# Layer 0 attention: three in five head pairs' probabilities transposed in fp32 on TensorE, stages of the pipeline reordered

## The chip, the cores and the metric

The kernel runs on one core of one Trainium2 chip. The metric is the device time of one execution in microseconds (us). A run's profile adds a trace of one execution: every instruction of TensorE (PE, with its weight loads as PEld), VectorE (DVE), ScalarE (ACT), GpSimd (POOL) and SyncE (SP, which here only issues DMAs), and the DMA packets.

## The reference, cut to what matters

Two layers of a diffusion backbone over 1024 latent tokens and 256 context tokens, width 1024. Layer 0 mixes by windowed attention with a sink (A, 8 heads, 2 key heads) and by 2-D neighbourhood attention (B, 8 heads); layer 1 by two other attentions; each layer ends in a mixture of experts. The change touches only the softmax and the value product of layer 0:

```python
s_ctx = einsum(q, k_c) * scale                      # 256 context keys
s_loc = einsum(q, k_local) * scale (+ bias in B)    # masked local keys
p_ctx, p_loc = joint_softmax([s_ctx, s_loc])        # in A also the sink's score
o = einsum(p_ctx, v_c) + einsum(p_loc, v_local)
```

The result has to be near to fp32, so the kernel keeps a number as two fp16 numbers, a high part and the rest (low part), and makes a product of three matmuls (high by high, high by low, low by high).

## The kernel before, in words

**Items.** `attn_l0` goes through six units: 0 and 1 are A with four heads each, 2 to 5 are B with two heads each. An item is one block of 128 queries of one head; a unit has 10 query blocks, so A has 80 items and B has 80. In A an item has 256, 512 or 640 keys, in B 256, 768 or 896 (256 of them context). Two neighbouring heads of a block are a pair: 80 pairs in all.

**One item's way** (`attn_unit`). `qk` (L679 to L682): scores into a PSUM buffer S of 1024 fp32; there are two (`ps_s`). `soft` (L702 to L730): maximum on DVE, exponentials on ACT into Pt (fp32, SBUF, two buffers), then their fp16 high part into Ps by an ACT copy (L730). `low` (L737): the low part, Pt minus high, into Ps; `low_eng` gives 4 items in 10 to POOL and 6 to DVE. After the second head of a pair, one DMA transposes all of Ps (high and low of both heads) into PT, issued by SP (L739). `pv` (L183 to L185 in `mm3`): three matmuls a key block, PT by values, into O; after a block's last head, DVE multiplies O by the reciprocal sums (L771), and ACT, POOL and a DMA store it.

**Order.** `pipelined` lets an item enter each step: at step i it emits qk of item i, pv of i-5, low of i-2 and soft of i-1. Beside it `interleave` emits the next unit's projection (`proj_unit`: products into ps_proj, its own DMA transposes at L628), the layer's modulation products (`ada`: L314, L317, L331), and B's bias tables (L502); in unit 5 instead of the projection the output mixer (`py`). The Tile framework's scheduler then sets a fixed order on each engine from this and from what depends on what; on the chip every engine goes through its row in that order, and an instruction that waits holds all behind it.

**DMA.** One hardware queue, issued by SP, carries weight loads and all transposes.

Of the kernel before, what the change touches and what calls it, by code (L numbers as in the profile page):

```python
# [12 lines left out]
F32 = mybir.dt.float32  # L13
# [55 lines left out]
def drain(g):  # L69
    for _ in g:  # L70
        pass


def pipelined(items, stages):
    n, depth = len(items), len(stages)
    st = [None] * n
    for i in range(n + depth - 1):
        for s in (0, *range(depth - 1, 0, -1)):
            j = i - s
            if 0 <= j < n:  # L80
                st[j] = stages[s](items[j], st[j])
        yield
# [362 lines left out]
def attn_l0(K, moe):  # L445
    nc, tc = K.nc, K.tc
    with ExitStack() as outer:
# [5 lines left out]
        ps_o = K.pool("l0pso", 2, PSUM, ctx)  # L453
# [55 lines left out]
        with ExitStack() as c0:  # L509
# [11 lines left out]
            for half, groups in ((0, ((8, 2, 1),)), (1, ((8, 2, 1), (0, 4, 0), (4, 4, 0)))):  # L521
                drain(K.ada([(0, half), (0, 2 + half)], wa, ps_p, 8, 3, 2, ps_o))
# [109 lines left out]
        def attn_unit(u):  # L632
# [53 lines left out]
            def soft(it, S):  # L686
# [14 lines left out]
                if isA:  # L701
# [4 lines left out]
                    nc.scalar.activation(Pt[:, :nk], S[:, :nk], AF.Exp, bias=nmh, scale=ESC,  # L706
                                         accum_out=dd[:, 0, h:h + 1])
                else:
# [10 lines left out]
                    nc.vector.tensor_scalar(nmh, mm, -ESC, LNSP, op0=ALU.mult, op1=ALU.add)  # L719
                    nc.scalar.activation(Pt[:, nl:nk], S[:, nl:nk], AF.Exp, bias=nmh, scale=ESC,  # L720
# [4 lines left out]
                if h % 2 == 0:  # L725
                    st_t[t, "Ps"] = pring.tile([P, 4 * 896], F16, name="Ps")
                    st_t[t, h] = tring.tile([P, 28, P], F16, name="PT")
                Ps, PT = st_t[t, "Ps"], st_t[t, h - h % 2]
                a = (h % 2) * 2 * nk
                nc.scalar.activation(Ps[:, a:a + nk], Pt[:, :nk], AF.Copy)  # L730
                return Pt, Ps, PT, a, nk

            def low(it, s):
                Pt, Ps, PT, a, nk = s
                w = 2 * nk
                h = it[1]
                K.low_eng().tensor_sub(Ps[:, a + nk:a + w], Pt[:, :nk], Ps[:, a:a + nk])  # L737
                if h % 2:
                    nc.sync.dma_start_transpose(out=PT[:, :2 * w // P, :], in_=Ps[:, :2 * w])  # L739
                return PT[:, a // P:(a + w) // P]  # L740

            def pv(it, PT):
# [4 lines left out]
                if h == 0:  # L747
                    st_t[t, "O"] = ps_o.tile([P, nh, 64], F32, name="O")
                O = st_t[t, "O"]
# [33 lines left out]
            same = lambda i, s: s  # L783
            yield from pipelined(items, [qk, soft, low, same, same, pv])
# [1270 lines left out]
```

## Time and profile before

| | |
|---|---|
| median of the runs | 3305.45 us |
| fastest run | 3302.15 us |
| profiled execution | 3305.77 us |
| its span in the trace | 3304.0 us (1.8 us lie outside) |
| first scores of layer 0 to last exponentials | about 107 to 788 us, a fifth of the span |
| PE, DVE, ACT, POOL busy over the span | 2616.3, 2599.6, 1976.2, 1000.7 us |

A busy PE is not a PE at its peak: a matmul's row lasts until its result is out, while the next may have begun. "Idle before" is the time that an engine stood still ahead of a group, and the names behind the arrow are what ended it. Lines are those of the kernel before, except in the passages of the order of the changed kernel.

### The profile page before, as it was taken

What the parts mean: (1) busy time and instruction counts of PE and PEld (TensorE: products, weight loads), DVE (VectorE), ACT (ScalarE), POOL (GpSimd) and SP (SyncE); (2) the same over time, 40 slices, a digit from 0 to 9 for tenths busy, and PEclk for the clock granted to TensorE, in tenths of its full rate; (3) what the DMA queues carried; (4) which work ended last, traced back from release to release, by engine and by line L of the source; (5) the groups of instructions that cost most, each with busy time, mean ns of one, the idle gap of its engine ahead of it and who ended that gap; (6) DMA issues with size and microseconds to landing.
All of it is one profiled execution on the core that took longest, in us unless ns stands there. A gap on an engine that the chain in (4) does not pass through costs nothing. (4 is left out here: it accounts for less than half of the span.)

```text
span 3304.0 us, 74455 instructions
## 1 busy us (share of the span) xinstructions
PE 2616.3 (79%) x30127; PEld 1777.7 (54%) x30127; DVE 2599.6 (79%) x4496; ACT 1976.2 (60%) x2949; POOL 1000.7 (30%) x652
## 2 busy tenths in 40 slices
PE   7888889968579989897467777877868579988886
PEld 3545445434267777775245555554534367776662
DVE  6777777778887768887667776778877897889987
ACT  5557777654456656676345655556653565656664
POOL 0123233232342212121432232222221463234443
PEclk8989999979789999999679998999978689999998
DMA  7789898789769889998648999655457589999996
GB/s 238 165 170 190 188 211 186 167 204 221 245 242 336 324 325 367 362 383 328 205 108 148 171 161 183 127 101 101 102 134 201 192 324 343 354 361 379 383 378 255
DMA packets 879159, 790.05 MB, mean 239 GB/s; under 512 B 689397, under 2 KB 719365, under 8 KB 878805
## 3 DMA queue, kind: packets, MB, share of 16 engines
q1 hardware_dynamic: 846981, 714.26, 74.9%
q0 software_dynamic: 26336, 69.85, 6.4%
q8 instruction: 239, 3.92, 0.5%
q10 hardware_dynamic: 5488, 1.09, 0.2%
q14 instruction: 115, 0.94, 0.1%
HBM read 565.85 MB, written 64.55 MB: 191 GB/s over the span
## 5 line engine op out<-in xcount | busy, mean ns | idle before, releaser
L375 DVE SCALAR_TENSOR_TENSOR arena<-arena 128x2048 f16<-128x2048 f32 (+4 forms) x439 | 917.8, 2112 | 175.1 <-ACT arena L374 165.6
L374 ACT ACTIVATE arena<-arena 128x2048 f16<-128x2048 f32 (+4 forms) x439 | 748.7, 1725 | 318.3 <-DMA arena<-in_w_gate_up_dram 195.0
L1364 PE MATMUL pg<-arena 128*128 128x72 f16 (+4 forms) x4736 | 633.3, 210 | 102.8 <-DVE arena L1351 80.4
L1366 PE MATMUL pg<-arena 128*128 128x72 f16 (+4 forms) x4736 | 629.9, 210 | 23.1 <-DVE arena L375 20.3
L1365 PE MATMUL pg<-arena 128*128 128x72 f16 (+4 forms) x4736 | 631.0, 210 | 14.8 <-DVE arena L1351 7.3
L183 PEld LDWEIGHTS <-arena 128*128 128x128 f16 (+1 forms) x3488 | 344.3, 103 | 341.0 <-DMA arena<-arena 128.4
L1365 PEld LDWEIGHTS <-arena 128*128 128x128 f16 x4736 | 473.0, 102 | 69.9 <-issue 66.0
L1366 PEld LDWEIGHTS <-arena 128*128 128x128 f16 x4736 | 472.4, 102 | 52.5 <-DVE arena L375 31.6
L1364 PEld LDWEIGHTS <-arena 128*128 128x128 f16 x4736 | 473.0, 102 | 34.0 <-ACT arena L374 21.4
L184 PEld LDWEIGHTS <-arena 128*128 128x128 f16 (+1 forms) x3488 | 344.3, 103 | 188.0 <-issue 96.2
L1381 POOL DMA_INDIRECT y_d<-arena,rt_sidx x74 | 233.9, 3161 | 615.8 <-ACT arena L1394 310.0
L185 PEld LDWEIGHTS <-arena 128*128 128x128 f16 (+1 forms) x3488 | 344.4, 103 | 129.0 <-issue 22.2
L183 PE MATMUL O<-arena 128*128 128x64 f16 (+1 forms) x1744 | 229.0, 208 | 129.9 <-DMA arena<-arena 98.6
L185 PE MATMUL O<-arena 128*128 128x64 f16 (+1 forms) x1744 | 228.7, 208 | 0.0
L184 PE MATMUL O<-arena 128*128 128x64 f16 (+1 forms) x1744 | 228.4, 208 | 0.0
L1774 POOL TENSOR_TENSOR arena<-arena 128x1280 f16<-128x1280 f32 x57 | 151.6, 2660 | 246.3 <-issue 174.8
L1755 ACT ACTIVATE arena<-S,arena 128x1280 f32<-128x1280 f32 x128 | 169.2, 1322 | 92.8 <-DVE arena L1753 80.6
L1344 POOL DMA_INDIRECT arena<-h_d,rt_gidx x74 | 144.2, 1948 | 233.4 <-PE pt L1350 173.1
L1752 DVE TENSOR_REDUCE arena<-S 128x1 f32<-128x1280 f32 x128 | 189.5, 1482 | 27.4 <-PE S L185 16.6
L195 PE MATMUL py<-arena 128*72 128x512 f16 (+4 forms) x592 | 184.1, 392 | 19.3 <-ACT arena L1376 14.2
L197 PE MATMUL py<-arena 128*72 128x512 f16 (+4 forms) x592 | 182.6, 390 | 0.0
L199 PE MATMUL py<-arena 128*72 128x512 f16 (+4 forms) x592 | 180.6, 386 | 0.0
(390 smaller groups left out, 6262.8 us busy)
## 6 DMA issues: line engine op xcount, KB each, us to landing
arena<-in_w_gate_up_dram SPq DMA_DIRECT2D x256, 1024.0 KB
arena<-in_w_down_dram SPq DMA_DIRECT2D x128, 1024.0 KB
arena<-in_w_ada_dram SPq DMA_DIRECT2D x96, 512.0 KB
arena<-y_d SPq DMA_DIRECT2D x36, 512.0 KB
x_d<-arena POOLq DMA_DIRECT2D x18, 512.0 KB, 3.5
h_d<-arena SPq DMA_DIRECT2D x18, 512.0 KB
arena<-x_d SPq DMA_DIRECT2D x18, 512.0 KB
arena<-in_x_dram SPq DMA_DIRECT2D x16, 512.0 KB
```

The source lines that it names most:

```text
L183: mm(ps, lh, rh, start=first, stop=False)
L184: mm(ps, lh, rl, start=False, stop=False)
L185: mm(ps, ll, rh, start=False, stop=last)
L195: mm(ps[:, o], lh, rh[:, o], start=first, stop=False)
L197: mm(ps[:, o], lh, rl[:, o], start=False, stop=False)
L374: nc.scalar.activation(wh, raw, AF.Copy, scale=scale)
L375: nc.vector.scalar_tensor_tensor(wl, raw, scale, wh, op0=ALU.mult, op1=ALU.subtract)
L1364: mm(pg[:, m, :n], wh, xh, start=k == 0 and m % 4 == 0, stop=False)
L1365: mm(pg[:, m, :n], wh, xl, start=False, stop=False)
L1366: mm(pg[:, m, :n], wl, xh, start=False, stop=k == 7 and m % 4 == 3)
L1381: self.K.nc.gpsimd.indirect_dma_start(out=self.K.y_d[self.l], out_offset=bass.IndirectOffsetOnAxis(ap=sidx, axis=0), in_=y[:n], in_offset= ...
L1752: nc.vector.reduce_max(mx[:, 0:1], S[:, :TOK], axis=AX.X)
```

## The change

Of every five pairs two keep the DMA (`by_dma`), three are transposed by TensorE: `turn` writes the transposes of Pt, in fp32, over the item's own scores in S; `high` copies S to PT as fp16 on ACT; `low` subtracts, on DVE, the high part from S and writes the low part to PT. In the pairs that keep the DMA, low is on POOL always. `soft` is cut in two, `peak` (maximum) and `soft` (exponentials), and the steps are emitted in a new order: at step i transposes of i-1, qk of i, pv of i-4, high of i-1, peak of i, low of i-1, soft of i. O is no longer a ring of two tiles but two halves of one tile (`sums`); the modulation's transposes have a pool of their own (`ps_t`).

```diff
@@ attn_l0
-        ps_o = K.pool("l0pso", 2, PSUM, ctx)
+        ps_t = K.pool("l0pst", 1, PSUM, ctx)
+        sums = K.pool("l0pso", 1, PSUM, ctx).tile([P, 2, 4, 64], F32, name="O")
...
-            def soft(it, S):
+            def peak(it, S):
...
-                    nc.scalar.activation(Pt[:, :nk], S[:, :nk], AF.Exp, bias=nmh, scale=ESC,
-                                         accum_out=dd[:, 0, h:h + 1])
...
+                return S, Pt
+
+            def soft(it, s):
+                S, Pt = s
...
+                if isA:
+                    nc.scalar.activation(Pt[:, :nk], S[:, :nk], AF.Exp, bias=nmh, scale=ESC,
+                                         accum_out=dd[:, 0, h:h + 1])
+                else:
...
                 if h % 2 == 0:
+                    st_t[t, h] = tring.tile([P, 28, P], F16, name="PT")
+                PT, a = st_t[t, h - h % 2], (h % 2) * 2 * nk
+                if not by_dma(it):
+                    return S, Pt, None, PT, a, nk
+                if h % 2 == 0:
                     st_t[t, "Ps"] = pring.tile([P, 4 * 896], F16, name="Ps")
...
+            def by_dma(it):
+                pair = (u * NT * nh + items.index(it)) // 2
+                return pair * 4 % 10 < 4
+
+            def turn(it, s):
+                S, Pt, Ps, PT, a, nk = s
+                if Ps is None:
+                    for j in range(0, nk, P):
+                        nc.tensor.transpose(S[:, j:j + P], Pt[:, j:j + P], K.id32)
+
+            def high(it, s):
+                S, Pt, Ps, PT, a, nk = s
+                if Ps is None:
+                    nc.scalar.activation(PT[:, a // P:(a + nk) // P].rearrange("p a n -> p (a n)"), S[:, :nk], AF.Copy)
 
             def low(it, s):
-                Pt, Ps, PT, a, nk = s
+                S, Pt, Ps, PT, a, nk = s
                 w = 2 * nk
-                h = it[1]
-                K.low_eng().tensor_sub(Ps[:, a + nk:a + w], Pt[:, :nk], Ps[:, a:a + nk])
-                if h % 2:
-                    nc.sync.dma_start_transpose(out=PT[:, :2 * w // P, :], in_=Ps[:, :2 * w])
+                if Ps is None:
+                    h_, l_ = (PT[:, (a + b) // P:(a + b + nk) // P].rearrange("p a n -> p (a n)") for b in (0, nk))
+                    nc.vector.tensor_sub(l_, S[:, :nk], h_)
+                else:
+                    nc.gpsimd.tensor_sub(Ps[:, a + nk:a + w], Pt[:, :nk], Ps[:, a:a + nk])
+                    if it[1] % 2:
+                        nc.sync.dma_start_transpose(out=PT[:, :2 * w // P, :], in_=Ps[:, :2 * w])
...
             def pv(it, PT):
...
-                if h == 0:
-                    st_t[t, "O"] = ps_o.tile([P, nh, 64], F32, name="O")
-                O = st_t[t, "O"]
+                O = sums[:, order.index(t) % 2, :nh]
...
-            same = lambda i, s: s
-            yield from pipelined(items, [qk, soft, low, same, same, pv])
+            n, st = len(items), {}
+            for i in range(n + 4):
+                if 0 < i <= n:
+                    turn(items[i - 1], st[i - 1])
+                if i < n:
+                    st[i] = qk(items[i], None)
+                if i >= 4:
+                    pv(items[i - 4], st.pop(i - 4))
+                if 0 < i <= n:
+                    high(items[i - 1], st[i - 1])
+                if i < n:
+                    st[i] = peak(items[i], st[i])
+                if 0 < i <= n:
+                    st[i - 1] = low(items[i - 1], st[i - 1])
+                if i < n:
+                    st[i] = soft(items[i], st[i])
+                yield
```

The program has 476 transposes of 128x128 more on PE and 48 DMA transposes fewer (32 of 80 stay). How the fixed order moves, at three places; "waits" names the engines or DMA queues whose semaphores a row waits for.

PE in unit 0. Before, scores of an item (L679, L680, the mask at L682) stand between projection products and wait for ACT, whose exponentials free the score buffer:

```order
L679 MATMUL S<-arena 128x256 [waits Activation_49]
L680 LDWEIGHTS arena
L680 MATMUL S<-arena 128x256
L679 LDWEIGHTS arena
L679 MATMUL S<-arena 128x256
L680 LDWEIGHTS arena
L680 MATMUL S<-arena 128x256
L682 LDWEIGHTS idbf
L682 MATMUL S<-amask,idbf 128x128
```

Now the transposes of two items (L759) stand there, each group behind a wait for ACT, then the value products into O (L183):

```order
L183 MATMUL ps_proj<-arena 128x384
L759 MATMUL S<-id_61,arena 128x128 [waits Activation_49]
L759 MATMUL S<-id_61,arena 128x128 x4
L184 LDWEIGHTS arena
L184 MATMUL ps_proj<-arena 128x384
L759 MATMUL S<-id_61,arena 128x128 [waits Activation_49]
L759 MATMUL S<-id_61,arena 128x128 x4
L185 LDWEIGHTS arena
L185 MATMUL ps_proj<-arena 128x384
L183 LDWEIGHTS arena
L183 MATMUL O<-arena 128x64
```

Further on in unit 0 a block's first value product waits for DVE, and so do scores (L681, L682 are the score lines now):

```order
L183 LDWEIGHTS arena [waits DMAHW2_49]
L183 MATMUL O<-arena 128x64 [waits DVE_49]
L184 LDWEIGHTS arena
L184 MATMUL O<-arena 128x64
L185 LDWEIGHTS arena
L185 MATMUL O<-arena 128x64
L183 LDWEIGHTS arena
L183 MATMUL O<-arena 128x64
L681 LDWEIGHTS arena
L681 MATMUL S<-arena 128x256 [waits DVE_49]
```

What moved: PE got two kinds of waits in every such item, for ACT ahead of the transposes and for DVE ahead of later scores. The first product into O has a wait for DVE in 32 of the 60 blocks (before: 3), and the multiply that it waits for is that of the block just before, since both halves of O count as one tile.

ACT in unit 0, before: exponentials (L706) and copies of the high part from SBUF (L730) in turn, two of the copies behind a DMA, which frees Ps:

```order
L706 ACTIVATE arena<-S,arena 128x640 [waits DVE_49,Pool_49]
L730 ACTIVATE arena<-arena 128x640 [waits DMAHW6_49,Activation_49]
L774 ACTIVATE arena<-arena 128x256 [waits DVE_49]
L706 ACTIVATE arena<-S,arena 128x640 [waits DVE_49]
L730 ACTIVATE arena<-arena 128x640 [waits Activation_49]
L706 ACTIVATE arena<-S,arena 128x640 [waits DVE_49,PE_49]
L730 ACTIVATE arena<-arena 128x640 [waits DMAHW7_49,Activation_49]
```

Now (L730 is the exponential, L764 the copy out of S, L746 the copy of a pair that keeps the DMA):

```order
L314 ACTIVATE arena<-arena 128x1024 [waits DMAHW2_49,PE_49]
L730 ACTIVATE arena<-S,arena 128x640 [waits DVE_49,Pool_49] x2
L764 ACTIVATE arena<-S 128x640 [waits DMAHW1_49,PE_49]
L764 ACTIVATE arena<-S 128x640 [waits PE_49]
L808 ACTIVATE arena<-arena 128x256 [waits DMASW2_49,DVE_49]
L730 ACTIVATE arena<-S,arena 128x640 [waits DVE_49,PE_49,Activation_49] x2
L617 ACTIVATE arena<-arena 128x4x64 [waits DMAHW0_49,DVE_49]
L764 ACTIVATE arena<-S 128x640 [waits PE_49]
L618 ACTIVATE arena<-arena 128x128
```

What moved: a copy that could run right behind its exponential now waits for PE's transposes, with the exponentials of both items of a pair ahead of it.

SP late in unit 0, before: every pair has its transpose (L739) between the modulation's loads (L310) and the projection's transposes (L628):

```order
L628 DMA_TRANSPOSE arena<-arena 128x6x128 [waits DMAHW2_49,DVE_49,Activation_49]
L339 DMA mod_d<-arena 2x512 [waits DVE_49]
L310 DMA arena<-in_w_ada_dram 128x2x512 [waits DMAHW4_49,DVE_49]
L739 DMA_TRANSPOSE arena<-arena 128x20x128 [waits DVE_49,DMAHW5_49,PE_49,Pool_49]
L310 DMA arena<-in_w_ada_dram 128x2x512 [waits DMAHW6_49,DVE_49]
L739 DMA_TRANSPOSE arena<-arena 128x20x128 [waits DMAHW0_49,DVE_49,DMAHW7_49,PE_49,Pool_49]
L628 DMA_TRANSPOSE arena<-arena 128x6x128 [waits DVE_49,Activation_49]
```

Now (L775 is the pair's transpose, L630 the projection's):

```order
L630 DMA_TRANSPOSE arena<-arena 128x6x128 [waits DMAHW5_49,DVE_49,Activation_49]
L310 DMA arena<-in_w_ada_dram 128x2x512 [waits DMAHW7_49,DVE_49]
L339 DMA mod_d<-arena 2x512 [waits DVE_49]
L310 DMA arena<-in_w_ada_dram 128x2x512 [waits DMAHW2_49,DMAHW0_49,DVE_49]
L630 DMA_TRANSPOSE arena<-arena 128x6x128 [waits DMAHW1_49,DVE_49,Activation_49]
L775 DMA_TRANSPOSE arena<-arena 128x20x128 [waits DMAHW4_49,PE_49,Pool_49]
L630 DMA_TRANSPOSE arena<-arena 128x6x128 [waits DMAHW3_49,DVE_49,Activation_49]
```

What moved: loads that stood behind a pair's transpose stand behind none for two or three pairs; the pair's transposes that stay wait for POOL alone where they waited for DVE or POOL.

## Rows read from the trace of the kernel before

**Rows 1.** Windows: stretch, length, busy us (count) by engine, clock, DMA share, GB/s.
```profile
core 0: us, PE busy (x) PEld busy (x) DVE busy (x) ACT busy (x) POOL busy (x), PEclk, DMA share, GB/s
60.00:68.80 8.80, 8.29 (x56) 5.77 (x55) 7.46 (x12) 8.43 (x14) 0.92 (x2) 0.96 0.45 120
107.00:788.00 681.00, 566.83 (x5447) 326.88 (x5446) 517.47 (x1277) 450.21 (x996) 212.04 (x224) 0.93 0.88 190
680.00:720.00 40.00, 21.71 (x182) 11.87 (x182) 26.17 (x70) 22.73 (x58) 12.74 (x14) 0.66 1.03 226
1000.00:1500.00 500.00, 448.54 (x7102) 365.87 (x7100) 383.99 (x268) 326.71 (x237) 107.83 (x61) 0.96 0.93 349
```

**Rows 2.** Maxima of A, B: count, ns shortest/median/longest, first and last start.
```profile
L702 DVE TENSOR_REDUCE arena<-S x80: 383/809/826, 109.2 to 370.8; 128x1 f32<-128x640 f32 x48, 128x1 f32<-128x512 f32 x16, 128x1 f32<-128x256 f32 x16
L709 DVE TENSOR_REDUCE arena<-S x80: 401/415/426, 373.9 to 779.1; 128x1 f32<-128x256 f32 x80
```

**Rows 3.** Pairs' DMA transposes: issue on SP (ns); waiters (us, times).
```profile
L739 SPq DMA_TRANSPOSE arena<-arena x80: 1231/3480/8281, 119.1 to 792.8; - x80
  PE O L183: 50.2, 31
  ACT arena L730: 25.5, 15
```

**Rows 4.** TensorE groups, 107 to 788 us: count, busy us, mean ns, idle before.
```profile
L183 PE MATMUL O<-arena 128*128 128x64 f16 x766 | 89.6, 200 | 48.6 <-DMA arena<-arena 48.3
L679 PE MATMUL S<-arena 128*128 128x256 f16 x224 | 60.8, 285 | 40.0 <-ACT arena L720 25.8 <-ACT arena L706 13.8
L183 PE MATMUL ps_proj<-arena 128*128 128x384 f16 x402 | 136.0, 338 | 7.4 <-DVE arena L625 3.2 <-ACT arena L505 2.6 <-DVE arena L337 1.6
```

**Rows 5.** Timeline, fp32 transposes (L417) among products: start us, length us.
```profile
60.51 0.73 PE L417 MATMUL ps_xt<-id,arena 128*128 128x128 f32 x4
61.07 0.33 PE L184 MATMUL ps_proj<-arena 128*128 128x384 f16 x1
61.24 0.60 PE L417 MATMUL ps_xt<-id,arena 128*128 128x128 f32 x4
61.67 0.33 PE L185 MATMUL ps_proj<-arena 128*128 128x384 f16 x1
61.84 0.33 PE L183 MATMUL ps_proj<-arena 128*128 128x384 f16 x1
```

**Rows 6.** DVE and ACT groups, layer 0: count, busy us, mean ns, idle before.
```profile
L737 DVE TENSOR_TENSOR arena<-arena 128x768 f16<-128x768 f32 x20 | 28.0, 1400 | 4.9 <-ACT arena L730 4.9
L737 DVE TENSOR_TENSOR arena<-arena 128x640 f16<-128x640 f32 x28 | 25.1, 898 | 4.1 <-ACT arena L730 2.4 <-issue 1.6
L702 DVE TENSOR_REDUCE arena<-S 128x1 f32<-128x640 f32 x48 | 39.0, 817 | 19.0 <-PE S L682 18.4 <-PE O L185 0.4
L771 DVE TENSOR_TENSOR arena<-O,arena 128x256 f32<-128x256 f32 x20 | 8.3, 417 | 2.0 <-PE O L185 1.9
L703 DVE TENSOR_SCALAR arena<-arena 128x1 f32<-128x1 f32 x68 | 13.3, 203 | 0.1
L705 DVE TENSOR_SCALAR arena<-arena 128x1 f32<-128x1 f32 x68 | 9.7, 144 | 0.3
L706 ACT ACTIVATE arena<-S,arena 128x640 f32<-128x640 f32 x48 | 37.7, 787 | 24.7 <-DVE arena L705 18.3 <-DVE arena L764 6.3
L706 ACT ACTIVATION_READ_ACCUMULATOR arena<-S,arena 128x1 f32 x80 | 15.6, 195 | 0.0
L730 ACT ACTIVATE arena<-arena 128x640 f16<-128x640 f32 x48 | 34.8, 734 | 9.7 <-DMA arena<-arena 9.1
```

**Rows 7.** Waits for score buffers, 116:372, then 660:800 us: us, times, longest.
```profile
PE S L679 <- ACT arena L706: 12.4, 14, 1.8
PE S L679 <- ACT arena L720: 24.2, 10, 6.4
```

More of the change, by code (lines that the diff above doesn't have):

```diff
@@ L521, in attn_l0 @@
             for half, groups in ((0, ((8, 2, 1),)), (1, ((8, 2, 1), (0, 4, 0), (4, 4, 0)))):
-                drain(K.ada([(0, half), (0, 2 + half)], wa, ps_p, 8, 3, 2, ps_o))
+                drain(K.ada([(0, half), (0, 2 + half)], wa, ps_p, 8, 3, 2, ps_t))
                 for t0, nb, w in groups:
@@ L719, in soft @@
                     nc.vector.tensor_scalar(nmh, mm, -ESC, LNSP, op0=ALU.mult, op1=ALU.add)
+                return S, Pt
+            def soft(it, s):
+                S, Pt = s
+                t, h = it
+                loc, cx = blocks(t)
+                nl, nk = len(loc) * P, (len(loc) + 2) * P
+                nm, dd = st_t[t]
+                nmh = nm[:, h:h + 1]
+                if isA:
+                    nc.scalar.activation(Pt[:, :nk], S[:, :nk], AF.Exp, bias=nmh, scale=ESC,
+                                         accum_out=dd[:, 0, h:h + 1])
+                else:
                     nc.scalar.activation(Pt[:, nl:nk], S[:, nl:nk], AF.Exp, bias=nmh, scale=ESC,
@@ L725, in soft @@
                 if h % 2 == 0:
+                    st_t[t, h] = tring.tile([P, 28, P], F16, name="PT")
[3 more added lines that the diff above has]
+                if h % 2 == 0:
                     st_t[t, "Ps"] = pring.tile([P, 4 * 896], F16, name="Ps")
-                    st_t[t, h] = tring.tile([P, 28, P], F16, name="PT")
-                Ps, PT = st_t[t, "Ps"], st_t[t, h - h % 2]
-                a = (h % 2) * 2 * nk
+                Ps = st_t[t, "Ps"]
                 nc.scalar.activation(Ps[:, a:a + nk], Pt[:, :nk], AF.Copy)
-                return Pt, Ps, PT, a, nk
+                return S, Pt, Ps, PT, a, nk
+            def by_dma(it):
[10 more added lines that the diff above has]
+                    nc.scalar.activation(PT[:, a // P:(a + nk) // P].rearrange("p a n -> p (a n)"), S[:, :nk], AF.Copy)
             def low(it, s):
-                Pt, Ps, PT, a, nk = s
+                S, Pt, Ps, PT, a, nk = s
                 w = 2 * nk
-                h = it[1]
-                K.low_eng().tensor_sub(Ps[:, a + nk:a + w], Pt[:, :nk], Ps[:, a:a + nk])
-                if h % 2:
-                    nc.sync.dma_start_transpose(out=PT[:, :2 * w // P, :], in_=Ps[:, :2 * w])
+                if Ps is None:
[5 more added lines that the diff above has]
+                        nc.sync.dma_start_transpose(out=PT[:, :2 * w // P, :], in_=Ps[:, :2 * w])
                 return PT[:, a // P:(a + w) // P]
```

## The prediction

> **What bounds the kernel now.** I read the busy shares by stretch first, then what one item's step costs, then who waits for the pairs' transposes, then the groups on each engine.
>
> Layer 0's attention runs from 107 to 788 us. In these 681 us PE is busy 567, DVE 517, ACT 450, and the DMA engines 0.88 of the time, at 190 GB/s [rows 1]. No engine is full and none has much room: the stretch is set by short waits between four parties in turn. For comparison, at 1000 to 1500 us the DMA engines move 349 GB/s at a share of 0.93, twice as much per busy time [rows 1]; so what fills them in layer 0 is not bytes but the transposes. PE idles 681 - 567 = 114 us there. Of that, 48 us are waits of the value products for a transposed pair, and 40 us waits of scores for a free buffer [rows 4]. Over the whole of the attention, value products wait 50.2 us for the pairs' transposes, in 31 waits, and ACT 25.5 us for Ps, which the same transposes set free [rows 3].
>
> An item of A comes every (370.8 - 109.2) / 79 = 3.31 us, one of B every (779.1 - 373.9) / 79 = 5.13 us [rows 2]. The rest of the span, 2600 us, holds nothing that the change edits. Its order shifts in places, and I cost that at nothing: the same instructions, with the same partners.
>
> I sum against the profiled execution, 3305.8 us, which is 0.3 us over the median of the runs shown.
>
> **The change, part by part.**
>
> *Transposes on PE.* 476 are added. The nearest rows are layer 0's fp32 transposes of the input between fp16 products: the next product begins 0.56 us after one group of four began, and 0.43 us after another [rows 5]. That is (0.56 + 0.43) / 8 = 0.124 us each, so 59 us; with the one or the other alone 51 or 67. How much of it falls into time in which PE stands still anyway? Without the waits for DMA 114 - 48 = 66 us of idle time are left, a good part of it while PE waits for ACT or DVE, which is when transposes of another item can run. But a transpose waits for ACT as well, so not all fits. I take 34 covered (ends 0 and 59), hence 25 on the path.
>
> *DMA transposes.* 48 of 80 go. By count 30 of the 50.2 us of PE's waits go with them; that is the one end, all 50 the other. For the rest I ask how full the DMA engines stay. Their work is 0.88 x 681 = 599 us. An estimate from the rows: 129 MB move (190 GB/s x 681 us); pairs' transposes are 51 MB of that (1568 blocks of 32 KB) and the projection's 12 MB; the other 66 MB at 349 / 0.93 = 375 GB/s take 177 us. So 63 MB of transposes take 422 us, and the 31 MB that move to PE take 208. The share falls from 0.88 to about 0.57, and most waits of the pairs that stay should go too: -42. ACT's waits for Ps lie mostly inside the same stalls: -8 (ends 0 and -25). On SP 48 issues of 3.5 us at the median go [rows 3], and the weight loads and projection transposes behind them come sooner; nothing on the path waits for those long, so 0.
>
> [...]
>
> *Copies and subtractions.* Both keep their number. On ACT an exponential of 640 read from S takes 787 ns, a copy of 640 from SBUF 734 [rows 6]; copies from S lie between a little more and a little less: 0 (ends -3 and +5). On DVE the 96 subtractions now read S. From SBUF those of 640 take 898 ns and those of 768 1400; from PSUM a maximum of 640 takes 817 and a product of 256 takes 417 [rows 6], so about 1.04 ns an element, 950 for 768. By that slope over all 96 it is 11 us less busy time on an engine that isn't the last to arrive: -4 (ends 0 and -11). POOL keeps 64, two in a row instead of spread; DVE and the next Pt wait for that a little, 0.
>
> *Scores held longer.* Before, S came free after the exponentials. Now in three of five pairs it holds until DVE has read the transposes. In A the way of one buffer is, with no wait in between: scores about 0.8 us, maximum and two small steps 0.82 + 0.20 + 0.14, exponentials 0.79 + 0.20, five transposes 0.62, copy 0.73, subtraction 0.82 [rows 6]: 5.1 us. Two buffers at 3.31 us an item allow 6.6. So 1.5 us are left for six hand-overs, where 3.7 were left before. In B, by the longest item's 896 keys for 640, the way is about 5.1 x 1.4 = 7.2 us of 10.3. PE already waits 12.4 us for S in A, where the buffer came free early, and 24.2 us in unit 5 [rows 7]. I take +10; ends are 0 and the 72 us of the rival below.
>
> *O as one tile.* In 32 of 60 blocks the first value product waits for the multiply of the block just before, 417 ns in A [rows 6], plus what stands ahead of it on DVE. Scores, projection and modulation products stand between on PE: +5 (ends 0 and 25).
>
> **Sum**: 59 - 34 - 42 - 8 - 4 + 10 + 5 = -14, so 3292 us. What is late next is the chain from scores over DVE and ACT back to PE.
>
> **The rivals.**
>
> *Scores bound A (slower).* Each hand-over from one engine to the next may wait behind that engine's other work: one instruction of the kinds in [rows 6] takes 0.2 to 1.4 us. If the six hand-overs wait more than (6.6 - 5.1) / 6 = 0.25 us each on average, the two buffers set A's pace. At 0.5 us an item takes (5.1 + 3.0) / 2 = 4.05 us, 0.75 more than now, and 48 items of A give +36 us; the waits of B add some 10. That makes 3292 + 46 = 3338; at 0.75 us a hand-over 1.5 us an item, +72 in A alone, and 3375 with B. For it: the fixed order puts a wait for ACT ahead of every group of transposes and a wait for DVE ahead of many scores, and PE holds everything behind them. Against it: B has 3 us of slack, and DMA pairs, two in five, free S as early as before. Chance 0.24.
>
> *DMA sets the pace (faster).* If nearly all of PE's idle time goes back to the full DMA queue, through late loads and late pairs, the stretch shrinks to PE's own work, 567 + 59 = 626 of 681 us: 3251. This floor is soft, since a PE row lasts 0.33 us where the next starts 0.16 us later [rows 5], so each break in the stream counts some latency as work; half of this case lies below 3240. For it: the share of 0.88, and 1.03 at 680 to 720 us, where PE is busy 22 of 40 us [rows 1]. Against it: only 48 of PE's 114 idle us end on a transpose. Chance 0.17.
>
> *The waits stay.* Both low parts of a DMA pair now stand behind each other on POOL, and the transposes that stay start later; were each to save nothing, -42 and -8 go: 3342. Chance 0.07.
>
> *The clock falls.* [...] The trace speaks against it, chance 0.04. [...]
>
> **How the numbers follow.** The forecast has 0.48; its own terms spread it over 3265 to 3320. For the range I take in the whole of it, the upper half of the DMA case, and the score case up to 3365: 3240 to 3365. Left out are half of the DMA case and a tail of the forecast below (0.10), and the top of the score case with the tails of the two small ones above (0.09). Two per cent is 66 us, about what can be told from no change here; that is below 3240 or above 3372. So faster by over 2%: 0.10; slower by over 2%: 0.08; within: 0.82.
>
> **What would show it.** Right: PE's idle time on the pairs' transposes under 12 us, the DMA share of the attention near 0.57, transposes 0.11 to 0.14 us apart, maxima of A every 3.2 to 3.4 us and of B every 4.9 to 5.1. The score rival shows as A over 3.7 us an item, with PE idle ahead of L681 on DVE and ahead of L759 on ACT. The DMA rival shows as B under 4.7 us. The forecast is wrong if the stretch from first scores to last exponentials leaves 640 to 710 us, or if the rest of the span moves by more than 10 us, which I cost at nothing.

## The result and the profile after

The changed kernel takes 3356.8 us (median of five runs, 3333.1 to 3360.0) against 3305.5: ratio 1.0141, 95% interval [1.0104, 1.0178]. That is 51 us slower where 13 us faster was forecast; it lies inside the range given and under 2%, but its interval leaves out no change. The profiled execution took 3333.1 us, the shortest of the five and 24 us under the median; a second one, shown further down, took 3351.4. So what the first profile shows is some 27 of the 51 us.

The stretch from the first to the last maximum of layer 0 can be read in every kernel, so I measure the attention by it. Maxima of A and of B in the changed kernel, columns as in [rows 2]:

```profile
L704 DVE TENSOR_REDUCE arena<-S x80: 403/815/826, 110.7 to 387.9; 128x1 f32<-128x640 f32 x48, 128x1 f32<-128x512 f32 x16, 128x1 f32<-128x256 f32 x16
L709 DVE TENSOR_REDUCE arena<-S x80: 399/418/426, 391.6 to 810.1; 128x1 f32<-128x256 f32 x80
```

An item of A comes every (387.9 - 110.7) / 79 = 3.51 us, one of B every 5.30: 0.20 and 0.17 more than in [rows 2]. The stretch is 699.4 us against 669.9 there, 29.5 more. What is left of the span, 3331.4 - 699.4 = 2632.0, is 2.1 us less than before. So between these two executions the whole loss lies in the attention. The same stretch by windows, first of the kernel before, then of the changed one, with the stretch of [rows 1] ahead:

```profile
109.20:779.10 669.90, 557.34 (x5334) 320.95 (x5332) 506.37 (x1251) 445.12 (x986) 208.96 (x221) 0.93 0.88 190
```

```profile
core 0: us, PE busy (x) PEld busy (x) DVE busy (x) ACT busy (x) POOL busy (x), PEclk, DMA share, GB/s
107.00:788.00 681.00, 589.33 (x5658) 360.27 (x5657) 497.93 (x1223) 433.63 (x966) 206.47 (x218) 0.96 0.58 139
110.70:810.10 699.40, 606.95 (x5819) 369.78 (x5818) 516.45 (x1256) 443.74 (x988) 213.07 (x223) 0.96 0.59 140
```

PE is busy 49.6 us longer and idle only 20.1 us less (112.6 to 92.4). The DMA engines did become free, 0.88 to 0.59. Who waits for the pairs that still go by DMA, to be read beside [rows 3]:

```profile
L775 SPq DMA_TRANSPOSE arena<-arena x32: 1237/3062/5673, 120.7 to 810.9; - x32
  PE O L183: 29.4, 21
```

And PE's waits at value products, scores and the new transposes, beside [rows 4]:

```profile
L183 PE MATMUL O<-arena 128*128 128x64 f16 x784 | 91.2, 198 | 33.4 <-DMA arena<-arena 29.4 <-ACT arena L764 2.8 <-DVE arena L805 0.9
L681 PE MATMUL S<-arena 128*128 128x256 f16 (+2 forms) x368 | 98.2, 285 | 24.3 <-DVE arena L771 7.8 <-ACT arena L733 6.4 <-ACT arena L730 4.3
L759 PE MATMUL S<-id,arena 128*128 128x128 f32 x476 | 76.3, 294 | 21.4 <-ACT arena L736 11.7 <-ACT arena L730 6.9 <-ACT arena L733 1.2
```

Before, 31 of 80 pairs were waited for, 1.6 us each; now 21 of 32 are, 1.4 us each. The share of late pairs went up from 39% to 66% on DMA engines that are a third emptier. The scores' waits fell by 16 us, and the transposes' own wait for the exponentials, 20 us, took their place.

### The profile page after: what moved, and what is told of

It is laid out like the page before. It is cut to its first block, busy times and chain, and to the rows that moved or that the text cites. A ratio compares the mean times of both kernels' runs of the same rounds, so it can differ in the third digit from the quotient of the medians.

```text
span 3331.4 us, 75205 instructions
## 1 busy us (share of the span) xinstructions
PE 2666.1 (80%) x30603; PEld 1826.0 (55%) x30603; DVE 2607.8 (78%) x4496; ACT 1971.8 (59%) x2949; POOL 1044.1 (31%) x652
## 5 line engine op out<-in xcount | busy, mean ns | idle before, releaser
L375 DVE SCALAR_TENSOR_TENSOR arena<-arena 128x2048 f16<-128x2048 f32 (+5 forms) x439 | 920.0, 2121 | 165.7 <-ACT arena L374 156.3
L183 PEld LDWEIGHTS <-arena 128*128 128x128 f16 (+1 forms) x3488 | 342.9, 102 | 316.3 <-DMA arena<-arena 105.8
L1414 PEld LDWEIGHTS <-arena 128*128 128x128 f16 x4736 | 471.9, 102 | 70.9 <-issue 66.1
L1415 PEld LDWEIGHTS <-arena 128*128 128x128 f16 x4736 | 471.3, 102 | 50.7 <-DVE arena L375 29.5
L1413 PEld LDWEIGHTS <-arena 128*128 128x128 f16 x4736 | 472.0, 102 | 32.1 <-ACT arena L374 18.4
L1430 POOL DMA_INDIRECT y_d<-arena,rt_sidx x74 | 255.6, 3454 | 572.1 <-ACT arena L1443 287.4
L185 PEld LDWEIGHTS <-arena 128*128 128x128 f16 (+1 forms) x3488 | 343.1, 102 | 130.8 <-issue 19.7
L183 PE MATMUL O<-arena 128*128 128x64 f16 (+1 forms) x1744 | 226.9, 207 | 111.6 <-DMA arena<-arena 78.8
L1393 POOL DMA_INDIRECT arena<-h_d,rt_gidx x74 | 169.4, 2289 | 228.9 <-PE pt L1399 163.0
L185 PE MATMUL O<-arena 128*128 128x64 f16 (+1 forms) x1744 | 225.8, 207 | 1.3 <-DVE arena L771 1.3
L184 PE MATMUL O<-arena 128*128 128x64 f16 (+1 forms) x1744 | 225.9, 207 | 0.0
L195 PE MATMUL py<-arena 128*72 128x512 f16 (+4 forms) x592 | 185.3, 394 | 20.9 <-ACT arena L1425 13.5
```

The source lines that it names most:

```text
L183: mm(ps, lh, rh, start=first, stop=False)
L184: mm(ps, lh, rl, start=False, stop=False)
L185: mm(ps, ll, rh, start=False, stop=last)
L195: mm(ps[:, o], lh, rh[:, o], start=first, stop=False)
L375: nc.vector.scalar_tensor_tensor(wl, raw, scale, wh, op0=ALU.mult, op1=ALU.subtract)
L1413: mm(pg[:, m, :n], wh, xh, start=k == 0 and m % 4 == 0, stop=False)
```

## The experiments

Notes for the table: "PE" is how many pairs in five are transposed by PE; "lead" by how many items the value products are emitted behind the scores; "O" whether the sums are one tile or a ring of two. The stretch runs from first to last maximum in the profiled execution; PE busy and idle are of that stretch, the rest is span minus stretch. The attention, by which the expectations go, runs from the first scores to the end of the last value product, 20 to 39 us more than the stretch; its last part, behind the last maximum, is counted in the rest. The waits are PE's for pairs by DMA over the whole attention (us / times). The first two rows are the kernel before and the changed kernel.

| order | PE | lead | O | median us | ratio to before, 95% | stretch | attention | PE busy / idle | pairs | rest |
|---|---|---|---|---|---|---|---|---|---|---|
| old | 0 | 5 | two | 3305.5 | 1 | 669.9 | 698.3 | 557 / 113 | 50.2 / 31 | 2634 |
| new | 3 | 4 | one | 3356.8 | 1.0141 [1.0104, 1.0178] | 699.4 | 726.9 | 607 / 92 | 29.4 / 21 | 2632 |
| the same again | 3 | 4 | one | 3357.7 | 1.0157 [1.0140, 1.0174] | 706.7 | 736.6 | 610 / 97 | 33.7 / 21 | 2643 |
| new | 3 | 5 | one | 3317.8 | 1.0037 [1.0024, 1.0051] | 670.4 | 698.2 | 599 / 71 | 15.4 / 14 | 2639 |
| new | 0 | 4 | one | 3318.8 | 1.0038 [1.0023, 1.0053] | 697.2 | 717.3 | 569 / 128 | 51.9 / 37 | 2625 |
| new | 0 | 5 | one | 3291.6 | 0.9960 [0.9945, 0.9975] | 663.1 | 690.9 | 549 / 115 | 40.6 / 27 | 2622 |
| new | 1 | 5 | one | 3309.2 | 1.0004 [0.9993, 1.0014] | 672.4 | 700.6 | 573 / 100 | 32.0 / 17 | 2639 |
| new | 2 | 5 | one | 3327.0 | 1.0061 [1.0044, 1.0078] | 694.2 | 716.9 | 593 / 101 | 31.1 / 16 | 2631 |
| old | 0 | 4 | two | 3346.2 | 1.0117 [1.0091, 1.0143] | 705.0 | 730.5 | 582 / 123 | 67.2 / 39 | 2636 |
| old | 0 | 6 | two | 3314.8 | 1.0030 [1.0016, 1.0044] | 666.8 | 700.1 | 546 / 121 | 43.9 / 30 | 2642 |
| new | 3 | 4 | two | 3354.1 | 1.0147 [1.0118, 1.0175] | 709.7 | 739.6 | 614 / 96 | 32.1 / 20 | 2640 |
| new | 3 | 5 | two | 3330.2 | 1.0080 [1.0060, 1.0101] | 683.9 | 711.7 | 600 / 84 | 24.7 / 19 | 2642 |
| new | 0 | 4 | two | 3315.0 | 1.0025 [1.0009, 1.0041] | 694.9 | 716.4 | 568 / 127 | 64.0 / 44 | 2624 |
| new | 0 | 5 | two | 3302.4 | 0.9978 [0.9964, 0.9992] | 675.1 | 703.2 | 555 / 120 | 54.7 / 35 | 2629 |
| new | 0 | 6 | two | 3302.4 | 0.9992 [0.9980, 1.0005] | 662.3 | 701.1 | 549 / 113 | 23.0 / 16 | 2638 |
| new, each transpose twice | 3 | 4 | one | 3381.0 | 1.0233 [1.0207, 1.0258] | 732.7 | 762.7 | 650 / 83 | 29.6 / 16 | 2639 |
| new, transposes late in the step | 3 | 5 | one | 3308.1 | 1.0006 [0.9991, 1.0021] | 666.0 | 693.8 | 598 / 68 | 8.6 / 10 | 2654 |

**The lead.** My first theory: the new order shortens the way from scores to value products by an item, from five to four, and so the pairs that stay with the DMA come late however empty its engines are. Averaged over the items (matched by order), from an item's maximum to its first value product there were 15.7 us in A and 23.0 in B before, 11.7 and 18.7 after. The experiment gives the item back:

```diff
-            for i in range(n + 4):
+            for i in range(n + 5):
...
-                if i >= 4:
-                    pv(items[i - 4], st.pop(i - 4))
+                if i >= 5:
+                    pv(items[i - 5], st.pop(i - 5))
```

> The changed kernel, with the value products of an item placed five items behind its scores instead of four (before the change they stood five behind). Theory, lead: the change shortened the way from an item's scores to its value products by one item (3.5 us in A), so the pairs that still go by DMA arrive late: PE waited for 21 of 32 of them, 29.4 us. One item more should leave under 8 us of such waits, and the attention of layer 0 and the whole should get 12 to 22 us shorter than the changed kernel's (3335 to 3345 against its median of 3357). Rival, load: the transposes arrive late because the DMA engines are loaded; then the waits stay at 20 us or more and the time within 6 us of 3357. Rival, moved: the waits go but come back ahead of the scores and the transposes (PE's score waits up by 10 us or more), and the time stays.

It took 3317.8 us, 39 less than the changed kernel and more than any of the theories had. PE's waits in it:

```profile
PE O L183 <- DMA arena<-arena: 15.4, 14, 1.8
PE S L681 <- DVE arena L771: 12.1, 12, 3.1
PE S L759 <- ACT arena L736: 6.7, 12, 2.0
PE S L759 <- ACT arena L730: 6.5, 12, 2.1
```

The waits for pairs halve (expected: under 8 us), those of the transposes fall from 19.8 to 13.5, those of the scores stay. The stretch is 670.4 us and the attention 698.2, those of the kernel before.

Then the same item taken from the kernel before (and, with one `same` more instead, one given to it):

```diff
-            yield from pipelined(items, [qk, soft, low, same, same, pv])
+            yield from pipelined(items, [qk, soft, low, same, pv])
```

> The kernel before with one empty stage fewer: value products four items behind the scores instead of five, nothing else of the change. Theory, lead: the same loss comes back without the change: the attention of layer 0 grows from 698 us by 15 to 40 us, PE's waits for pairs from 50.2 us to over 75, and the time is 3320 to 3345. Rival, plan: what the runs showed as the lead is the program's order being planned anew, which moved other kernels by 12 us either way; then this lies at 3294 to 3318.

> The kernel before, all pairs by DMA, with one empty stage more: value products six items behind the scores instead of five. Theory, lead: the 31 waits for pairs (50.2 us) are only a matter of how early a pair's probabilities are ready; an item more (3.3 us in A, 5 us in B) against a wait of at most 3.4 us leaves under 10 us of them, and the time falls by 20 to 45 us, to 3260 to 3285, with no work on PE added. Rival, load: the DMA engines set the pace of the pairs; the queue is then as long whatever the lead, the waits stay at 35 us or more and the time within 8 us of 3305.

With four items the kernel before takes 3346.2 us, just over the 3345 that the theory had at most: nearly the whole loss of the change, with none of its other edits. Maxima and PE's waits there:

```profile
L702 DVE TENSOR_REDUCE arena<-S x80: 394/811/826, 111.4 to 378.9; 128x1 f32<-128x640 f32 x48, 128x1 f32<-128x512 f32 x16, 128x1 f32<-128x256 f32 x16
L709 DVE TENSOR_REDUCE arena<-S x80: 396/416/426, 380.8 to 816.4; 128x1 f32<-128x256 f32 x80
```

```profile
PE O L183 <- DMA arena<-arena: 67.2, 39, 5.8
PE S L679 <- ACT arena L720: 23.3, 8, 6.4
PE S L679 <- ACT arena L706: 12.8, 15, 2.2
```

The waits for pairs grew by 17.0 us to 67.2 (over 75 were expected), but the stretch by 35.1. From an item's maximum to its first value product 15.0 us pass in A and 21.9 in B, only 0.7 and 1.2 less than with five items: the item that the order took away comes back as waiting. From the first scores to the last value product, PE's work is the same number of instructions and yet busy longer. Three windows each (A, B, tail) and their sums, of the kernel before, then with four items:

```profile
371.00:779.00 408.00, 341.21 (x3138) 187.72 (x3135) 302.23 (x713) 271.80 (x606) 132.02 (x138) 0.92 0.89 195
...
sum 698.00, PE 581.64 PEld 334.08 DVE 531.60 ACT 457.11 POOL 215.61; mean PE 193.88 PEld 111.36 DVE 177.20 ACT 152.37 POOL 71.87
```

```profile
379.00:816.00 437.00, 362.58 (x3190) 196.77 (x3189) 310.96 (x716) 272.46 (x607) 137.07 (x140) 0.89 0.83 183
...
sum 730.00, PE 603.51 PEld 343.80 DVE 537.27 ACT 455.74 POOL 220.44; mean PE 201.17 PEld 114.60 DVE 179.09 ACT 151.91 POOL 73.48
```

Counts over the three windows are 5581 and 5585 PE instructions; busy time is 22 us more, idle time 10 more. In B the granted clock is 0.89 where it was 0.92. So the shorter lead shows here twice, as idle time and as products that are slower; that the idle time brought on the lower clock is not shown.

With six items the old order gained nothing: 3314.8 us, the waits for pairs 43.9 us in 30. That is what the load theory had for the waits (35 or more), and the time is just past its 8 us. But the rings of buffers (three for PT, two for Ps) stayed as they were, so that they, and not the load, hold the pairs back is a rival that was not tried. A got quicker (3.16 us an item), B slower (5.23).

**What the new order and the transposes cost apart.** All pairs by DMA in the new order, with four and with five items:

```diff
-                return pair * 4 % 10 < 4
+                return pair >= 0
```

> The changed kernel with every pair by DMA: the new order of the stages and the sums as one tile, without a transpose on PE. Theory, lead: with four items instead of five between scores and value products most of the 80 pairs are late; PE waits for them more than before (over 90 us against 50.2), and the time is 25 to 80 us above the kernel before (3330 to 3385), as much as or more than the change itself costs. Rival, price: the loss of the change is PE's new work and the order costs nothing; then this kernel lies within 10 us of 3305.

> The changed kernel with value products five items behind the scores and every pair by DMA: the new order of the stages, but neither PE's transposes nor the shorter lead. Theory, lead: of the 14 us that the new order costs without a transpose on PE (3319 against 3305), nearly all is the item of lead; with it back this lies at 3300 to 3310 and the attention of layer 0 at 694 to 704 us (698 before, 717 without the item). Rival, rest of the order (sums as one tile, every subtraction on POOL, exponentials in their own step): 3314 or more, attention over 708 us.

With four items 3318.8 us, 13 above the kernel before: less than the lead theory's 25, more than the rival's 10; the waits for pairs are 51.9 us, not over 90. With five 3291.6, under what either expected, 0.4% faster than the kernel before. So the rest of the new order is no cost. It reads as a gain at the same lead in all four comparisons of the table (with one tile and two, with four items and five), by 0.002 to 0.009 of the time. PE's waits with four items, then with five:

```profile
PE O L183 <- DMA arena<-arena: 51.9, 37, 3.6
PE S L681 <- ACT arena L733: 26.1, 10, 5.3
PE S L681 <- ACT arena L730: 9.3, 9, 3.8
```

```profile
PE O L183 <- DMA arena<-arena: 40.6, 27, 4.1
PE S L681 <- ACT arena L730: 19.0, 18, 2.5
PE O L183 <- DVE arena L805: 18.8, 9, 8.1
PE S L681 <- ACT arena L733: 13.9, 11, 3.5
```

From this kernel the change can be put together by ratios: new order with five items -0.004 (-13 us), the item of lead +0.008 (+26), the transposes +0.010 to +0.012 (some +36), in all +0.014 to +0.016. In the attention it reads -7, +26 and +10 us (+19 in the second execution). The last value products with three in five by PE and with none, first with four items, then with five (the first scores begin at 109.2, 109.6, 107.5 and 109.4 us):

```profile
L185 PE MATMUL O<-arena x784: 191/193/261, 125.2 to 835.9; 128*128 128x64 f16 x196
L185 PE MATMUL O<-arena x784: 192/193/243, 126.2 to 826.6; 128*128 128x64 f16 x196
L185 PE MATMUL O<-arena x784: 191/193/261, 124.0 to 805.5; 128*128 128x64 f16 x196
L185 PE MATMUL O<-arena x784: 191/193/243, 127.7 to 800.2; 128*128 128x64 f16 x196
```

So the item of lead shows whole in the attention, but of the transposes' price only 10 to 19 us with four items and 7 with five (of 26 by the medians). The stretch alone misleads here: up to the last maximum the transposes seem to cost 2.2 us with four items, since without them less is left behind it (18.6 us against 25.9). Outside the attention the kernels with PE's transposes are 0 and 8 us longer with four items (two executions) and 18 with five. No instruction is edited there; two executions of the changed kernel alone differ there by 8 us, and the scheduler plans the order of the whole program anew. What that part of the price is was not tried and stays open.

The price of a transpose, by issuing each twice:

```diff
-                    for j in range(0, nk, P):
+                    for j in (*range(0, nk, P), *range(0, nk, P)):
```

> The changed kernel with each of the 476 transposes issued twice into the same place. Theory, price: PE is what the attention of layer 0 waits for, so that transposes lie on the path at nearly their full price: 476 more at 0.124 us add 45 to 60 us, 3400 to 3417 against 3357. Rival, cover: a good part (more than half) falls into PE's waits, as the prediction had it for 34 of 59 us; then under 30 us are added, below 3387.

24 us more by the medians, 26 to 33 in the stretch, where the theory had 45 to 60 and the rival under 30: about half of 59 us lies on the path. PE's row of the stretch:

```profile
109.80:842.50 732.70, 649.79 (x6308) 414.96 (x6306) 515.60 (x1258) 448.56 (x989) 212.08 (x223) 0.98 0.56 134
```

It is busy 43 us longer than in the changed kernel and idle 10 us less (83 against 92; 14 less than in the second execution). So idle time covered 10 to 14 of the 59 us. The clock went up again, 0.96 to 0.98.

Fewer pairs by PE, with five items: `pair * 6 % 10 < 6` (two in five) and `pair * 8 % 10 < 8` (one).

> Five items of lead, and two pairs in five transposed by PE instead of three. PE has about 160 transposes less (20 us at 0.124), the DMA engines 16 pairs more. Theory, PE's price: with the lead back the transposes lie on PE's path at most of their price, so the time falls by 8 to 18 us against five of lead with three in five (3318), to 3300 to 3310. Rival, DMA: more pairs by DMA are late again, PE's waits for pairs rise from 15 us to over 25, and the time stays at 3314 to 3325.

> Five items of lead, and one pair in five by PE (about 320 transposes less than three in five, 40 us of PE). Theory, PE's price: 3290 to 3305, below the kernel before, since a fifth less of the transposes' load on the DMA engines takes some of the waits for pairs (50 us before) for 20 us of work on PE. Rival, DMA: waits for pairs are back at 40 us or more and the time at 3303 to 3315, as with every pair by DMA.

A miss for the price theory: two in five is 9 us slower than three in five. Waits for pairs are 31 and 32 us in 16 and 17 waits, over the 25 that the rival had for two in five and under its 40 for one: about as many waits as with three in five (14), but longer ones. The time is 2 us over the rival's range for two in five and inside it for one. The times of none, one, two and three in five (3292, 3309, 3327, 3318) don't lie on a line; every split that uses PE is slower than none in the new order with five items.

**How far a plan of its own moves a kernel.** The changed kernel once more, and the kernels with two tiles of sums, `ps_o` in the place of `sums`:

```diff
-        ps_t = K.pool("l0pst", 1, PSUM, ctx)
-        sums = K.pool("l0pso", 1, PSUM, ctx).tile([P, 2, 4, 64], F32, name="O")
+        ps_t = K.pool("l0pst", 2, PSUM, ctx)
+        ps_o = ps_t
...
-                O = sums[:, order.index(t) % 2, :nh]
+                if h == 0:
+                    st_t[t, "O"] = ps_o.tile([P, nh, 64], F32, name="O")
+                O = st_t[t, "O"]
```

> The changed kernel once more, unaltered, on the chip of the runs beside it. Its first profiled execution (3333 us) lies 24 us under the median of its runs (3357). Theory, attention: the executions differ in the attention of layer 0, whose waits depend on when transposes land; a second profile of a longer execution shows first scores to last value products longer than the 727 us of the first, and the rest of the span within 8 us of 2489. Rival, elsewhere: the attention is again 725 to 730 us and a longer execution is longer in the expert layers. The median is expected at 3335 to 3360.

> Every pair by DMA, five items of lead, the new order of the stages (3292 us), and the sums again in a ring of two tiles as before the change, in place of one tile that holds both. Theory, one tile: the value products of a block that wait for the multiply of the block just before it (18.8 us in 9 waits of PE for VectorE with five items of lead) wait no more; the time falls by 5 to 18 us, to 3274 to 3287. Rival, moved: PE then waits for pairs or for the scores' buffers instead, and the time stays within 4 us of 3292.

> Three in five pairs by PE, five items of lead (3318 us), and the sums in a ring of two tiles. PE waited 5.8 us for VectorE ahead of value products there. Theory, one tile: 3312 to 3318; whatever the tile, the transposes keep it 20 us or more above the same kernel with every pair by DMA. Rival, PE covered: below 3305.

The second execution is 18 us longer, 7.3 in the stretch and 10.9 in the rest: neither theory alone. Two tiles took away what they were meant to take away, with every pair by DMA the waits for the multiply, 18.8 us; yet the kernels became 11 us (every pair by DMA) and 12 us slower by the medians. By the ratios it is 6 and 14 us, and in the first of the two the intervals meet. PE's waits with two tiles and every pair by DMA:

```profile
PE O L183 <- DMA arena<-arena: 54.7, 35, 3.5
PE S L681 <- ACT arena L733: 20.3, 12, 3.6
PE S L681 <- ACT arena L730: 13.6, 16, 1.9
```

The waits moved to the pairs (40.6 to 54.7), as the rival had it, though not within its 4 us. With three in five by PE the time is over the theory's 3318, but its other half held: 28 us above the same kernel with every pair by DMA. Nothing here excludes that it is the new plan and not the tile. So a difference of some 12 us between two kernels is not by itself the work of the edit, and I repeated the step of the lead under these plans:

> The changed kernel (four items, three in five pairs by PE) with two tiles of sums. With five items it took 3330 us (attention 712). Theory, lead: 25 to 42 us more with four, 3355 to 3372, attention 735 to 755. Rival, plan: within 14 us of 3330.

> Every pair by DMA, four items, two tiles of sums. With five items it took 3302 us (attention 703). Theory, lead: 15 to 35 us more, 3317 to 3337, attention 718 to 738. Rival, plan: within 14 us of 3302.

> Every pair by DMA, the new order, two tiles of sums, and six items of lead. PE still waited for pairs for 40.6 us (27 times) with five. Theory, lead: one more item (3.3 us in A) takes most of them, 5 to 20 us less than with five. Rival, load: with every pair by DMA (DMA engines busy 0.88 of the attention before) the pairs come at the pace of the DMA engines; as with the kernel before, where six items gave 10 us more than five, the time is equal or up to 12 us longer than with five.

From five items to four: +24 us with three in five by PE (just under what was expected), +13 with none, under the theory's 15 and inside the band of the rival. Six items gave nothing over five with every pair by DMA (3302.4 both); the waits for pairs fell to 23.0 us, and those for score buffers took over, 53.2 us. (In that kernel the ring for the sums of the exponentials is one short for six items, so in B a block is divided by a later block's sums; the time is read for the order of the work only.) Over all five pairs of kernels the item from four to five is worth 0.005 to 0.012 of the time, always with the same sign, and the attention 13 to 38 us. Together with the old order, where nothing else was edited, I take the cost of the lead for shown, though not its size for any one plan. PE's waits for pairs make up 7 to 18 us of it; the remainder is other idle time and longer busy time of PE, whose cause is not shown.

**Transposes late in the step**: with five items, `turn` moved behind `pv`, right ahead of `high`.

> Three in five pairs by PE, five items of lead, and the transposes of an item placed behind the value products of its step instead of ahead of the next scores. Theory, too early: PE's waits for exponentials ahead of transposes (13.5 us in 26) are a matter of place; behind the value products they fall under 4 us, and the time falls by 5 to 12 us, to 3306 to 3313. Rival, buffers: the scores' buffer comes free later by the same work, PE's waits ahead of scores (22.9 us) grow by 10 us or more, and the time is 3316 or more.

```profile
PE S L759 <- ACT arena L730: 9.2, 14, 1.9
PE O L183 <- DMA arena<-arena: 8.6, 10, 1.4
PE S L681 <- DVE arena L771: 8.1, 10, 3.5
PE S L759 <- ACT arena L736: 7.6, 7, 3.1
```

3308.1 us, in the range of the theory, but not by its way: the transposes wait 17.6 us for the exponentials, not under 4, and the scores' waits didn't grow. Its profiled execution was the longest of ten (3322.0 us, with a rest of 2654), so the gain can't be told from the plan's part.

## Why the prediction was wrong, by its steps

| step of the sum | forecast | measured |
|---|---|---|
| transposes on PE | +59 | price right: five in 0.60 us, 0.12 each; PE busy +50 in the stretch |
| of it covered by idle time | -34 | idle time other than for pairs 65.9 us before, 66.1 after: none net |
| waits for pairs | -42 | -21 (50.2 to 29.4; in the stretch 46.7 to 26.3) |
| ACT's waits for Ps | -8 | the 25.5 us are gone, replaced: copies from S wait 34.2 us for PE |
| subtractions on DVE | -4 | sizes right: 952 ns for 768 (950), 819 for 640 |
| scores held longer | +10 | waits for S -16, new waits of the transposes +20 |
| O as one tile | +5 | 0.9 us of waits for L805 (18.8 with every pair by DMA and five items) |

**Two steps failed.** The first is "most waits of the pairs that stay should go too: -42". Its premise, the load, was sized well: the DMA share of [rows 1] fell to 0.58 where 0.57 was forecast, and pairs that are waited for land 5.1 us after their issue on average where they took 6.5 before. But the wait was read as queueing alone. The diff says that value products move from five items behind to four; the description of the change names it, and the prediction priced nothing for it. With the item given back, PE's waits for pairs in the stretch are 15.4 us (-31), and the attention is that of the kernel before.

The second is "I take 34 covered", a choice between 0 and 59 for which no row gave the size. With the smaller terms, idle time other than for pairs was to fall by 34 + 8 + 4 - 10 - 5 = 31 us; it stayed, because the transposes brought waits of their own (20 us) where those of the scores fell (16). With the item given back it is 55.5 us (-10). So the sum would not have come out even then: 42 us more of busy PE against 42 us less of idle PE.

In the first profiled execution the two make up the miss: idle time fell by 20 us instead of 73, 21 short in the waits for pairs and 31 in the other idle time, while PE's busy time grew by 50 instead of 59. About 21 of the missing 53 us come back with the lead. The further 18 us of the second execution, 10 in the attention and 8 outside, no term accounts for.

Transposes among products, beside [rows 5] (start, length):

```profile
166.40 0.76 PE L759 MATMUL S<-id,arena 128*128 128x128 f32 x5
167.00 0.33 PE L184 MATMUL ps_proj<-arena 128*128 128x384 f16 x1
167.18 0.77 PE L759 MATMUL S<-id,arena 128*128 128x128 f32 x5
167.78 0.33 PE L185 MATMUL ps_proj<-arena 128*128 128x384 f16 x1
```

The subtractions and copies that read S on the changed kernel, as in [rows 6]:

```profile
L771 DVE TENSOR_TENSOR arena<-S,arena 128x640 f16<-128x640 f32 x28 | 22.6, 819 | 18.7 <-ACT arena L764 18.6
L771 DVE TENSOR_TENSOR arena<-S,arena 128x768 f16<-128x768 f32 x16 | 15.2, 952 | 3.5 <-ACT arena L764 3.5
```

```profile
L764 ACT ACTIVATE arena<-S 128x640 f16<-128x640 f32 x28 | 19.4, 701 | 14.0 <-PE S L759 13.9
L764 ACT ACTIVATE arena<-S 128x640 f16<-128x640 f32 (+4 forms) x96 | 66.4, 696 | 35.0 <-PE S L759 34.2
```

One reading in the prediction was off, without weight in the sum: the bytes per busy time at 1000 to 1500 us are 1.7 times those of layer 0 (349 / 0.93 against 190 / 0.88), not twice.

*Its rivals.* Score buffers bounding A: A at 3.51 us an item lies between the forecast's 3.4 and the rival's 3.7, and the idle time that it named is there (L681 on DVE, L759 on ACT), so this rival had the sign. But it is not the cause: scores wait less than before, and with the item of lead given back, where S is held by the same steps, A is at (374.5 - 108.9) / 79 = 3.36 us. DMA setting the pace: B did not get quicker. "The waits stay" (3342): half of the 42 us stayed, but not because transposes start later. From the second maximum of a pair that keeps the DMA to the end of its issue on SP 8.8 us pass in A and 10.3 in B, where 10.6 and 12.6 passed before (averages); from there to its first value product 2.3 and 3.7 us, where there were 2.9 and 6.3. It is the end of the way that came closer. The clock: it rose, from 0.93 to 0.96 over the stretch, and no run with transposes among the products there shows one under 0.93. What transposes would cost at a lower clock, no run shows. Over 60 to 68.8 us, where 24 fp32 transposes of the input (L417) stand among the products in both kernels, the clock was 0.96 before and 0.79 after, so that window alone speaks neither for this rival nor against it.

*Its own tests* passed in part: DMA share and spacing right; waits for pairs (29.4 against under 12) and both item times wrong. First scores to last exponentials take 705 us in the first execution and 712 in the second, across the limit of 710; the rest of the span beside them moved by 2 and 13 us, across the limit of 10. So neither of these two tests would have told by the first execution alone.

## What to carry to other kernels

Before pricing a resource that a change relieves, count the steps between producer and consumer before and after: here PE's waits for pairs fell only from 50.2 to 29.4 us while the DMA share fell from 0.88 to 0.59, and an item less of lead cost 13 to 41 us by the medians, where the work that was added cost 26 to 39. Cover by idle time is to be sized from rows too, for the new work brought waits of its own here (20 us). Test the parts of such a change alone; here the reordering with the old lead and no transposes was the only part worth keeping (ratio 0.996 with one tile, 0.998 with two). Where every edit plans the whole program anew, a difference of some 12 us needs a second plan before it is put down to the edit.

## What the runs showed of the hardware

The clock granted to TensorE was higher in the kernels with two pairs in five or more transposed among the products. In the stretch it was 0.91 to 0.94 in the eight executions without a transpose on PE (0.93 before), 0.93 with one pair in five, 0.95 with two, 0.95 to 0.97 in the six with three, and 0.98 with each transpose doubled, 952 of them. How full PE was does not order it alone: 0.91 with four items of lead in the old order (PE busy 582 of 705 us), 0.94 with six (546 of 667), nearly the same share. Where the clock was higher the products were quicker: those of the projection take 330 ns at 0.96 in the changed kernel, 338 at 0.93 before [rows 4], and 344 at 0.91 with four items in the old order. By an estimate from these means, over some 405 products at each of L183 to L185, PE's busy time is 10 us less by this in the changed kernel, against the transposes' price, and 7 us more with four items in the old order, on top of the shorter lead's. The rows of the changed kernel, then of the old order with four items:

```profile
L183 PE MATMUL ps_proj<-arena 128*128 128x384 f16 x405 | 133.7, 330 | 11.6 <-ACT arena L507 4.4 <-DVE arena L627 4.1 <-DVE arena L337 2.7
L183 PE MATMUL ps_proj<-arena 128*128 128x384 f16 x406 | 139.8, 344 | 8.1 <-ACT arena L505 5.3 <-DVE arena L625 1.7 <-DVE arena L719 0.4
```

Taking 48 DMA transposes out lowered the share of the DMA engines by 0.29 to 0.30 (0.88 to 0.59 over the stretch) while bytes fell from 190 to 140 GB/s; between kernels of the new order that differ in nothing else it fell from 0.83 to 0.59 (four items) and from 0.89 to 0.62 (five).
